# Hybrid encoder layer on one core: the first four row tiles in a hand-written order, seven idle products, a gain row spread over 97 partitions, one weight cast moved, and the last residual kept in PSUM

## The chip, the cores and the metric

The kernel runs on one core of a Trainium2 chip. A core has a matrix engine (TensorE, PE in the profile, with its weight loads listed apart as PEld), a vector engine (VectorE, DVE), an activation engine (ScalarE, ACT), a general engine (GpSimd, POOL) and a queue engine that mostly issues transfers (SyncE, SP). Products are written into PSUM, eight banks of 128 partitions; all else lies in SBUF. Each engine executes its own instructions strictly in the order in which the program lists them for it, and waits on semaphores of the others; transfers are issued from the queues of SP, ACT and POOL. The metric is the device time of one execution in microseconds (us).

## The reference, cut to what matters

```python
n = rms_norm(x, mix_norm_g)
proj = n @ w_in                      # 512 x 4608
...                                  
h = x + merged @ w_out
h = h + memory_cross_attention(rms_norm(h, xattn_norm_g), memn, w_q, w_k, w_v, w_xo)
h = h + (silu(hn @ w_gate) * (hn @ w_up)) @ w_down      # hn = rms_norm(h, ffn_norm_g)
return rms_norm(h, final_norm_g)
# rms_norm(x, g) = x * rsqrt(mean(x*x, -1) + 1e-6) * g
```

There are 512 token rows of 1024 float32 numbers. `proj` is cut into an S5 branch, a gated branch with GELU and layer norm, and two sigmoid gates. The change touches the first line (the norm of `x`, and the first 512 columns of the product that feed the gated branch), the load order at `w_xo` and `w_gate`, and the last line.

## The kernel before, in words

**Tiles and halves.** The 512 rows are four row tiles of 128 (`NT`), the 1024 features eight blocks of 128 (`KD`). Each float32 operand of a product is split in two: `hi`, a copy rounded to fp32r (a CAST on ACT), and `lo`, the source minus `hi` (a TENSOR_TENSOR on DVE). A product is three matmuls (`mm3`, the matmul's line is L360): hi by hi, hi by lo, lo by hi. So a weight tile costs a transfer into `wraw` (three buffers), a cast `whi` on ACT and a difference `wlo` on DVE (L85 and L86 for all of them, three buffers each) before PE can use it.

**What sets the order.** `plan` is the list of all weight tiles in the order of their use. `next_w` takes the next one and thereby issues loads some tiles ahead (`LOADS` 3) and splits two tiles ahead (`SPLITS` 2). Around this, a scheduler arranges each engine's instructions by its own estimate of when each can run, except where `tc.keep_in_program_order` (`in_order`) pins an instruction to its place in the program. `side` holds the S5 branch as a generator (`s5_program`, with the parameter set-up in `s5_setup`, L622), of which `tick` gives out pieces between products.

**The first rows.** Six idle products of `ones` by `ones` (L558) run on PE first. `mix_norm_g` arrives as one row on one partition (`g_row`), and a product of a single row of `ones` with it spreads it over 128 partitions into PSUM (`pg`, L581); ACT copies it to SBUF (`g_mix`). A row tile `xt` is squared and summed in two halves on ACT (`sum_sq`, L486), the factor is made by two small DVE operations and a power on POOL (`rms_factor`, L495 to L497), DVE scales the tile (L585 for the first tile, L512 for the others), PE transposes it in eight blocks (`to_feat`, L520) into `ptr`, and ACT and DVE split that into `xn`, the operand of all of stage one. Row tiles 1 to 3 go through the same steps in a loop. Then `tokm(w_in, OFF_V, ...)` (L1031) runs over four weight tiles of `w_in`, each two feature blocks by 512 columns, and all four row tiles: 96 matmuls into four banks `pt`. After it come the `feat` products (`pf`). The transfers stand on SP's queue in this order: the gain, half of row tile 0 (the other half on ACT's queue), the first weight tile, row tile 1, the second weight tile, row tile 2, the third, row tile 3; after them the S5 parameters, the first of which is `slab<-in_s_log_step_dram`, whose exponential stands at L674.

**w_xo and w_gate.** The second half of `w_xo` is four plan blocks of two feature blocks each; the first two use the ordinary `whi`/`wlo` buffers, the other two go to places `s2` and `s4`. Then `plan_units` takes the first block of the last 256 columns of `w_gate` into place `s1`, ahead of everything else that it plans. In the profile these casts read `s<-wraw`, and the sums on the rows that follow each product are L1348 on DVE and L486 on ACT.

**The end.** The last product of `w_down` (`dx`, quadrant 4) ends with row tile 3. `finish_last(None, ...)` adds what `dx[1]` holds to the residual `h` (L1806); the last three weight tiles are then multiplied in two column halves into a fresh bank `pcut`, each half is added to `h` on DVE (L1806 again), squared and summed (L486), and after the second the square root (L1788), the reciprocal (L1789), the scaling (L1819 on ACT, L1823 on DVE) and the two last transfers follow.

## Time and profile before

| | |
|---|---|
| device time, median of 3 executions | 871.61 us (870.81 to 874.23) |
| device time of the profiled execution | 871.84 us |
| its span, first to last instruction | 870.1 us, so 1.74 us lie around it |
| PE, PEld busy | 859.9 us (99%), 767.3 us (88%) |
| DVE, ACT, POOL busy | 660.9 us (76%), 464.5 us (53%), 92.3 us (11%) |
| moved by DMA | 169.56 MB, mean 195 GB/s |

The span counts from the first instruction of the program to the last. A busy PE is not PE at its peak: matmuls are pipelined, and the row of one shows its whole passage, 389 ns for 512 columns, while in an unbroken series one starts each 227 ns. In the timeline a row gives the start in us, the duration (of all, where several were merged, as x2), engine, line, operation, what is written `<-` what is read, the shape, and in brackets how long the engine had been idle and what ended that. A window row gives, for a stretch, its length and the busy time and count of each engine; with a source line it counts that line's instructions alone. A group row gives the count, the busy sum, the mean duration in ns and the idle time in front. The wait list gives total, times, longest.

### The profile page before, as it was taken

What the parts mean: (1) busy time and instruction counts of PE and PEld (TensorE: products, weight loads), DVE (VectorE), ACT (ScalarE), POOL (GpSimd) and SP (SyncE); (2) the same over time, 40 slices, a digit from 0 to 9 for tenths busy, and PEclk for the clock granted to TensorE, in tenths of its full rate; (3) what the DMA queues carried; (4) which work ended last, traced back from release to release, by engine and by line L of the source; (5) the groups of instructions that cost most, each with busy time, mean ns of one, the idle gap of its engine ahead of it and who ended that gap; (6) DMA issues with size and microseconds to landing.
All of it is one profiled execution on the core that took longest, in us unless ns stands there. A gap on an engine that the chain in (4) does not pass through costs nothing.

```text
span 870.1 us, 14734 instructions
## 1 busy us (share of the span) xinstructions
PE 859.9 (99%) x5766; PEld 767.3 (88%) x5766; DVE 660.9 (76%) x1072; ACT 464.5 (53%) x693; POOL 92.3 (11%) x127
## 2 busy tenths in 40 slices
PE   8999999999999999999999999999999999999996
PEld 6787888888889988889899878999999999988875
DVE  5699885999857768668758755867877768899875
ACT  5643953244356544547556554655545455656574
POOL 1002200301021210100010001001111111000010
PEclk9999999999999999999999999999999999999999
DMA  8769556797655898725686545557899998366672
GB/s 246 197 181 299 111 160 178 175 248 194 169 174 174 259 284 265 248 97 194 215 269 169 147 130 161 146 149 194 205 237 237 214 227 224 92 190 203 197 239 96
DMA packets 115464, 169.56 MB, mean 195 GB/s; under 512 B 9265, under 2 KB 80449, under 8 KB 115266
## 3 DMA queue, kind: packets, MB, share of 16 engines
q1 hardware_dynamic: 94722, 138.50, 48.5%
q0 software_dynamic: 20384, 29.60, 20.7%
q8 instruction: 45, 0.74, 0.3%
q10 hardware_dynamic: 288, 0.52, 0.2%
q14 instruction: 25, 0.20, 0.1%
HBM read 159.71 MB, written 48.73 MB: 240 GB/s over the span
## 4 chain that ended last, share of the span: by engine, by line
PE 95%; DMA 2%; DVE 1%; ACT 1%; SPq 1%; issue 0%; ACTq 0%; DVEq 0%
PE pf L360 26%; PE pt L360 16%; PE px L1158 13%; PE dx L360 6%; PE pq L1158 6%; PE dq L360 3%; PE pv L1158 3%; PE bx L1158 3%; PE qx L1158 3%; PE dv L360 2%; PE pz L892 2%; PE qv L1158 1%; PE po L360 1%; PE psc L360 1%; PE py L948 1%; PE qq L1158 1%
## 5 line engine op out<-in xcount | busy, mean ns | idle before, releaser
L85 ACT CAST whi<-wraw 128x1024 fp32r<-128x1024 f32 (+1 forms) x145 | 148.7, 1025 | 161.8 <-PE pf L360 51.4
L86 DVE TENSOR_TENSOR wlo<-wraw,whi 128x1024 fp32r<-128x1024 f32 (+1 forms) x145 | 172.1, 1188 | 60.5 <-ACT whi L85 59.7
L360 PE MATMUL pf<-xn,whi 128*128 128x512 f32 x448 | 140.2, 392 | 0.0
L360 PEld LDWEIGHTS pf<-xn,whi 128*128 128x128 f32 x448 | 83.7, 188 | 17.1 <-issue 0.2
L360 PE MATMUL pf<-xn,wlo 128*128 128x512 f32 x224 | 87.6, 392 | 0.0
L1158 PE MATMUL px<-fn,whi 128*128 128x256 f32 x480 | 83.4, 277 | 0.0
L1158 PEld LDWEIGHTS px<-fn,whi 128*128 128x128 f32 x480 | 72.5, 188 | 0.2
L86 DVE TENSOR_TENSOR wlo<-b,whi 128x1024 fp32r<-128x1024 f32 x40 | 48.9, 1222 | 26.1 <-ACT whi L85 26.0
L85 ACT CAST whi<-b 128x1024 fp32r<-128x1024 f32 x40 | 42.1, 1053 | 48.6 <-PE px L1158 27.8
L1158 PE MATMUL px<-fn,wlo 128*128 128x256 f32 x240 | 66.4, 277 | 0.0
L1158 PE MATMUL pq<-s,whi 128*128 128x256 f32 x320 | 55.0, 276 | 0.0
L360 PE MATMUL dx<-whi,s 128*128 128x512 f32 x166 | 52.2, 391 | 0.4 <-DVE h L1831 0.4
L86 DVE TENSOR_TENSOR wlo<-t,whi 128x1024 fp32r<-128x1024 f32 x30 | 36.7, 1224 | 18.4 <-ACT whi L85 18.4
L85 ACT CAST whi<-t 128x1024 fp32r<-128x1024 f32 x30 | 31.6, 1054 | 34.3 <-PE pv L1158 11.4
L360 PEld LDWEIGHTS pf<-xn,wlo 128*128 128x128 f32 x224 | 42.1, 188 | 8.8 <-issue 0.2
L1158 PEld LDWEIGHTS pq<-s,whi 128*128 128x128 f32 x320 | 48.2, 188 | 0.0
L360 PE MATMUL pt<-whi,xn 128*128 128x512 f32 x128 | 44.5, 414 | 1.3 <-ACT xn L85 1.1
L1158 PEld LDWEIGHTS px<-fn,wlo 128*128 128x128 f32 x240 | 45.1, 188 | 0.0
L1158 PE MATMUL pq<-s,wlo 128*128 128x256 f32 x160 | 44.2, 276 | 0.0
L360 PEld LDWEIGHTS dx<-whi,s 128*128 128x128 f32 x166 | 31.1, 188 | 7.4 <-issue 0.8
L360 PE MATMUL dx<-wlo,s 128*128 128x512 f32 x83 | 32.3, 391 | 0.1
L277 POOL DMA_DIRECT2D dsum<-in_w_down_dram x12 | 13.3, 1109 | 174.7 <-DMA dsum<-in_w_down_dram 171.0
(456 smaller groups left out, 2217.7 us busy)
## 6 DMA issues: line engine op xcount, KB each, us to landing
wraw<-in_w_in_dram SPq DMA_DIRECT2D x36, 512.0 KB, 4.8
dsum<-in_w_down_dram SPq DMA_DIRECT2D x20, 512.0 KB, 5.9
wraw<-dsum SPq DMA_DIRECT2D x20, 512.0 KB, 4.0
b<-in_w_gate_dram SPq DMA_DIRECT2D x15, 512.0 KB, 5.4
b<-in_w_up_dram SPq DMA_DIRECT2D x15, 512.0 KB, 4.8
wraw<-in_w_down_dram SPq DMA_DIRECT2D x15, 512.0 KB, 4.6
dsum<-in_w_down_dram POOLq DMA_DIRECT2D x10, 512.0 KB, 8.0
dsum<-dsum POOLq DMA_DIRECT2D x10, 512.0 KB, 8.6
```

The costliest lines, as they stand in the source:

```text
L85: hi = nc.scalar.copy(dst_hi, src)
L86: lo = nc.vector.tensor_tensor(dst_lo, src, dst_hi.bitcast(F32), ALU.subtract)
L277: plan[j + step][1].append((0, lambda d=dst, x=more: nc.gpsimd.dma_start(d, x, accum_op=ALU.add)))
L360: m = nc.tensor.matmul(ps, a[x], b[y], start=start and i == 0, stop=stop and i == 2, skip_group_check=free)
L892: nc.tensor.matmul(ps[:, g, :], wt[:, g, :], u[:, o * GO + g, :], start=True, stop=True)
L948: in_order(nc.tensor.matmul(ps[64 * j:64 * j + 64, :, :, h, :].rearrange("p q d c -> p d q c"), a, b, start=k == ks[0], stop=k == ks[2], t ...
L1158: nc.tensor.matmul(ps[:, j, :], a[x], b[y], start=start and j == k == i == 0, stop=k == 3 and i == 2, skip_group_check=True)
```

## The change

Four parts.

1. **First rows.** `first_rows` now builds all four row tiles from a hand-written string of steps, all pinned: `sq` squares a half, `ms` scales the first half's sum on DVE, `rt` takes the square root on ACT (the power on POOL is gone), `rc` the reciprocal on DVE, `sc` scales a half from the spread gain in PSUM, `pt` transposes four blocks, `hi` and `lo` split them, `whi` and `wlo` split half a weight tile, `p` is three matmuls of one row tile with one feature block of one of the first three weight tiles (`p121` is row 1, weight tile 2, block 1), `idle2` and `idle5` are two and five idle products. The gain arrives on partition 96 of a tile whose partitions 0 to 95 are set to zero, and is spread by a product of 97 rows. The first products run between the preparations; what `tokm` did is written out with the rest of them. The first two weight tiles are loaded in two halves each, and the third stands ahead of row tiles 2 and 3.
2. **S5 set-up.** The exponential of `log_step` is issued where the step is loaded.
3. **w_gate's first cast** gets a dependency in order alone on the cast of the second block of `w_xo`.
4. **The end.** The residual of the last row tile's right half is added to what `dx[1]` holds into two free banks `dv` (`seed_last`), the last products accumulate onto these, and squares and scaling read PSUM.

```diff
     def split(dst_hi, dst_lo, src):
...
+        return hi
...
-        split(hi, lo, src)
+        cast[0] = split(hi, lo, src)
         return hi, lo

+    cast = [None]
+
+    def behind(ins, first):
+        tc.add_manual_dep(ins.ins, first.ins.name, mybir.DependencyInfo(
+            mybir.DependencyClass.NoSync, mybir.DependencyReason.DATA), reason="order of the casts")
...
-            ins = nc.sync.dma_start(got["raw"], block(w, kb, k, c0, n))
-            if ordered:
-                in_order(ins)
+            for i in range(0, k, k // parts):
+                ins = nc.sync.dma_start(got["raw"][:, i:i + k // parts], block(w, kb + i, k // parts, c0, n))
+                if ordered:
+                    in_order(ins)
...
-            plan_block(w_gate, 4 * i, 4, FS, 256, place=i + 1, ordered=True)
+            plan_block(w_gate, 4 * i, 4, FS, 256, place=i + 1, ordered=True,
+                       then=None if i else lambda ins: behind(ins, xo_cast[0]))
...
-    plan_tok(w_in, OFF_V, KD)
+    plan_tok(w_in, OFF_V, KD, parts=2)
...
+    xo_cast = []
     for i in range(4):
-        plan_block(w_xo, 2 * i, 2, 512, 512, place=(None, None, 2, 4)[i], ordered=True)
+        plan_block(w_xo, 2 * i, 2, 512, 512, place=(None, None, 2, 4)[i], ordered=True,
+                   then=xo_cast.append if i == 1 else None)
...
-    idle = aux("idle", (P, P))
+    pg = [bank("pg") for i in range(2)]
+    pt = {t: bank(f"pt{t}") for t in range(NT - 1)}
...
-    nc.scalar.activation(warm, mhalf, AF.Square)
+    nc.scalar.activation(warm, ones[:, 0:1], AF.Sqrt)
...
+    G_ROW = 96
+    g_row = np_.tile([P, D], F32, tag="gain", name="g_row", bufs=2)
+    nc.vector.memset(g_row[0:G_ROW], 0.0)
+    in_order(nc.sync.dma_start(g_row[G_ROW:G_ROW + 1], mix_norm_g))
     nc.scalar.dma_start(xt[:, 0, HALF[1]], x[0:P, HALF[1]])
-    for t in range(1, NT):
-        load_raw(t - 1)
-        nc.sync.dma_start(xt[:, t, :], x[t * P:(t + 1) * P])
+    in_order(nc.sync.dma_start(xt[:, 0, HALF[0]], x[0:P, HALF[0]]))
+    for row, blocks in ((0, (0,)), (1, (1, 2)), (2, ()), (3, ())):
+        if row:
+            in_order(nc.sync.dma_start(xt[:, row, :], x[row * P:(row + 1) * P]))
+        for i in blocks:
+            load_raw(i)
...
+        def pg_(i):
+            in_order(nc.tensor.matmul(pg[i], ones[0:G_ROW + 1, :], g_row[0:G_ROW + 1, HALF[i]], start=True, stop=True))
+        def rt(t):
+            in_order(nc.scalar.activation(sums[t][:, 0:1], sums[t][:, 1:2], AF.Sqrt, bias=roots.pop(t), scale=1.0 / D))
...
+    ORDER = """
+        pg0 sq00 sq01 ms0 pg1 rt0 rc0 sc00 idle2 pt00 whi00 hi00 wlo00 whi01 lo00 sc01 sq10 idle5 p000 whi10
+        pt01 ms1 wlo01 sq11 wlo10 p001 rt1 whi11 rc1 p010 sc10 hi01 wlo11 pt10 whi20 sc11 hi10 p011 sq20 lo10
+        pt11 wlo20 p100 sq21 ms2 lo01 p101 rt2 sq30 rc2 sc20 p110 hi11 ms3 sq31 pt20 sc21 p020 hi20 lo11 pt21
+        whi21 lo20 p111 rt3 hi21 wlo21 p200 rc3 p021 sc30 p201 lo21 p120 sc31 pt30 p210 hi30 pt31 lo30 p211
+        hi31 bank3 p300 lo31 p121 p301
+    """
...
-        A_.activation(stp, ls, AF.Exp)
+        in_order(A_.activation(stp, ls, AF.Exp))
...
+    def seed_last(ps):
+        for i in range(2):
+            in_order(nc.vector.tensor_tensor(last[i], h[:, NT - 1, last_cols[i]], ps[:, 256 * i:256 * i + 256], ALU.add))
...
-    finish_last(None, dx[1])
+    seed_last(dx[1])
...
-        p = aux("pcut", (P, 256))
         for c, ops_ in held:
-            rows_product({1: p}, 4, c, ops_, (1,), slice(256 * i, 256 * i + 256), c == CHUNKS - HELD, c == CHUNKS - 1, True)
-        finish_last(i, p)
+            rows_product({1: last[i]}, 4, c, ops_, (1,), slice(256 * i, 256 * i + 256), False, c == CHUNKS - 1, True)
+        finish_last(i)
```

How this moves instructions is seen at three places. First PE at the program's start, before (L558 idle, L581 the spread of the gain, L520 transposes of `xt`, L360 products):

```order
L558 MATMUL idle<-ones 128x128 x6
L581 MATMUL pg<-g_row,ones 128x512 x2
L520 MATMUL ptr<-ident,xt 128x128 x8
L360 MATMUL pt_263<-whi,xn 128x512
L360 MATMUL pt_263<-wlo,xn 128x512
```

and now (L573 idle, L608 the gain, L635 transposes, L374 products; the idle products write the bank of the third `pt`):

```order
L573 MATMUL pt_111<-ones 128x128 x6
L608 MATMUL pg<-g_row,ones 128x512 x2
L573 MATMUL pt_111<-ones 128x128 x2
L635 MATMUL ptr<-ident,xt 128x128 x4
L573 MATMUL pt_111<-ones 128x128 x5
L374 MATMUL pt_109<-whi,xn 128x512
L374 MATMUL pt_109<-wlo,xn 128x512
L374 MATMUL pt_109<-whi,xn 128x512
L635 MATMUL ptr<-ident,xt 128x128 x4
```

The first products of row tile 0 now stand between the transposes of its two halves, and idle products fill the places ahead of the first transposes and of the first product.

Second, ACT at `w_xo`, before (L486 squares of a finished row tile; of the two `s` casts the second is `w_gate`'s; `whi<-wraw` is the second block of `w_xo`):

```order
L486 ACTIVATE sq,hss<-h 128x512 [waits DVE_49]
L85 CAST s_5468<-wraw 128x1024 [waits DMAHW0_49]
L85 CAST whi<-wraw 128x1024 [waits DMAHW2_49,PE_49]
L486 ACTIVATE sq,hss<-h 128x512 [waits DVE_49,Activation_49]
L85 CAST whi<-b_5447 128x1024 [waits DMAHW1_49,PE_49]
```

and now:

```order
L500 ACTIVATE sq,hss<-h 128x512 [waits DVE_49,Activation_49]
L85 CAST whi<-wraw 128x1024 [waits DMAHW4_49,PE_49]
L85 CAST s_5478<-wraw 128x1024 [waits DMAHW2_49]
L85 CAST whi<-b_5457 128x1024 [waits DMAHW3_49,PE_49]
L500 ACTIVATE sq,hss<-h 128x512 [waits DVE_49,Activation_49] x3
```

The two casts change places, and the squares of the third row tile come ahead of both.

Third, DVE at the end, before:

```order
L1806 TENSOR_TENSOR h<-h,dx_8067 128x512
L1866 TENSOR_TENSOR h<-h,dx_8066 128x512
L1789 RECIPROCAL r<-ms 128x1
L1823 SCALAR_TENSOR_TENSOR h<-h,r,g_o 128x512
L1806 TENSOR_TENSOR h<-h,pcut 128x256
L1774 SCALAR_TENSOR_TENSOR msq<-ss,msq 128x1
```

and now:

```order
L1890 TENSOR_TENSOR dv_8215<-h,dx_8077 128x256
L1890 TENSOR_TENSOR dv_8216<-h,dx_8077 128x256
L1950 TENSOR_TENSOR h<-h,dx_8076 128x512
L1869 RECIPROCAL r<-ms 128x1
L1908 SCALAR_TENSOR_TENSOR h<-h,r,g_o 128x512
L1854 SCALAR_TENSOR_TENSOR msq<-ss,msq 128x1
L1908 SCALAR_TENSOR_TENSOR h<-dv_8215,r,g_o 128x256
L1908 SCALAR_TENSOR_TENSOR h<-dv_8216,r,g_o 128x256
```

The two additions of `pcut` behind the last products are gone; one addition ahead of them became two of half the width, and the last scaling became two of half the width.

More of the change, by code (lines that the diff above doesn't have):

```diff
@@ L670, in s5_setup @@
         st["c"] = (cr, ci)
-        stp, a, rho, th, n, sn, hs, cs = (small() for _ in range(8))
-        A_.activation(stp, ls, AF.Exp)
+        a, rho, th, n, sn, hs, cs = (small() for _ in range(7))
         V.tensor_tensor(a, lr, stp, ALU.mult)
@@ L1822, in write @@
         (nc.gpsimd if t < 2 else nc.sync).dma_start(rows[:, cs], hg[:, t, :])
[L1823 to L1825 removed]
+        for src, cols in zip(last, last_cols) if t == NT - 1 else ((h[:, t, hs], hs),):
+            scaled = nc.vector.scalar_tensor_tensor(h[:, t, cols], src, r, g_o[:, cols], ALU.mult, ALU.mult)
+            if pinned[0]:
+                in_order(scaled)
         (nc.gpsimd, nc.gpsimd, nc.sync, nc.scalar)[t].dma_start(rows[:, hs], h[:, t, hs])
```

133 lines of the change are left out of this document (82 added, 51 removed).

## The prediction

> **What bounds the kernel now.** I read the chain of waits first, then PE's waits, then the stretches around them in the timeline. The chain's shares by engine:
>
> ```profile
> PE 95%; DMA 2%; DVE 1%; ACT 1%; SPq 1%; issue 0%; ACTq 0%; DVEq 0%
> ```
>
> The end is PE's list of instructions, so a change counts only where it shortens the work on PE, speeds it up, or removes one of PE's few stops. The largest stops, as total, times, longest:
>
> ```profile
> PE pt L360 <- ACT xn L85: 1.1, 1, 1.1
> PE pt L360 <- DVE wlo L86: 0.7, 1, 0.7
> ```
>
> The first lies in the first rows (17.34 below), the second at `w_xo` (520.22 below). All else that can be won is the speed of the first products and what stands behind the last one. For the speed, windows of L360 alone (length, PE busy and count, PEld, granted clock):
>
> ```profile
> 9.60:13.50 3.90, 3.85 (x8) 2.61 (x9) 1.00 1.05 349
> 18.10:22.00 3.90, 3.90 (x18) 3.19 (x17) 1.00 0.88 231
> 29.20:42.50 13.30, 10.69 (x43) 7.58 (x42) 1.00 0.63 149
> ```
>
> The granted clock is 1.00 in every row, yet 8 products fill 3.9 us in the first and 18 in the second: a product every 0.43 us (3.4/8) until about 13.5, every 0.22 to 0.23 afterwards. The clock column does not show this slowness; only the spacing does. I use 0.227 for the fast step and 0.427 for the slow one.
>
> **Part 1, the start.** The rows of before:
>
> ```profile
> 3.92 3.78 PE L581 MATMUL pg<-g_row,ones 1*128 1x512 f32 x4
> 4.25 0.63 ACT L486 ACTIVATE sq<-xt 128x512 f32<-128x512 f32 x1 [1.59 <-DMA xt<-in_x_dram]
> 6.72 0.75 DVE L585 SCALAR_TENSOR_TENSOR xt<-xt,r,pg 128x512 f32<-128x512 f32 x1 [0.76 <-ACT g_mix L583]
> 8.54 1.12 PE L520 MATMUL ptr<-ident,xt 128*128 128x128 f32 x4
> 9.65 0.80 PE L360 MATMUL pt<-whi,xn 128*128 128x512 f32 x1
> 15.16 1.03 PE L520 MATMUL ptr<-ident,xt 128*128 128x128 f32 x8
> 16.59 0.23 ACT L674 ACTIVATE slab<-slab 128x32 f32<-128x32 f32 x1 [0.58 <-DMA slab<-in_s_log_step_dram]
> 17.34 0.50 PE L360 MATMUL pt<-whi,xn 128*128 128x512 f32 x1 [1.15 <-ACT xn L85]
> 42.51 0.62 PE L360 MATMUL pf<-xn,whi 128*128 128x512 f32 x2
> ```
>
> From the first product (9.65) to the first `pf` (42.51) pass 32.9 us. The work in them, at the fast step: 96 products, 96 x 0.227 = 21.8. 24 transposes of rows 1 to 3: eight pass in 1.03, of which the last one's passage is about 0.27, so (1.03 - 0.27)/7 = 0.11 each, 2.6 together. The S5 set-up's small transposes: the third window is 13.3 long and 43 products take 9.8 of it, which leaves 3.5, and 3.8 with one that lies earlier. Sum 28.2. The other 4.7 us are the slow step until 13.5 (8 x 0.2 = 1.6), the stop of 1.15 at 17.34, where ACT stood with the exponential of the step (16.59, waiting for a transfer) ahead of the cast that PE needed, and small waits for weight tiles. All three are what the change addresses: products of row 0 begin between its transposes, PE is kept occupied ahead of them, and the exponential leaves ACT's first rows.
>
> What happens instead, by the list of steps. The gain still takes four passes of which one lasts about 0.85 (3.78 for four, overlapping): the half that `sc00` needs is ready near 6.0. Row 0's halves land at about 3.5 (2.8 after an issue at 0.75 on ACT's queue) and 4.2; the one that lands first is now squared first, so both are squared near 5.0, and with root and reciprocal (0.3 and 0.2) the factor is there near 5.5. So the gain decides: `sc00` starts near 6.1, 0.6 before the scaling at 6.72, since the copy into `g_mix` is gone. The idle products' price has a row:
>
> ```profile
> L558 PE MATMUL idle<-ones 128*128 128x128 f32 x12 | 2.9, 434 | 1.1 <-DVE mhalf L481 1.1
> ```
>
> Six of them (two passes each) cost 2.9 slow, 0.24 a pass; `idle2` and `idle5` are 4 and 10 passes: 0.9 and 2.4 slow, and at the fast spacing of a transposition (0.11) 0.4 and 1.1. They fill time in which PE would wait for the scaling and for the cast, so fast they cost nothing; slow, `idle5` stands up to 1 us in front of the first product. That is the first unknown: whether PE is fast at 7 or at 13.5.
>
> Fast from about 6.7 (my choice, because the spread is then 97 rows and not one, and PE is busy without gaps from about 1): the spread ends 7.1, `idle2` 7.5, four transposes 8.0, the cast of half a row 8.8 (0.6 for 512 columns), `idle5` covers to 9.05, first product 9.05. Then only row 0 and row 1 feed PE until row 2 arrives. Rows of `xt` land thus:
>
> ```profile
> 2.05 0.47 SPq L573 DMA_DIRECT2D xt<-in_x_dram  x1
> 3.07 0.47 SPq L573 DMA_DIRECT2D xt<-in_x_dram  x1
> DMA to landing us min/median/max: 2.8/7.2/11.4
> ...
> xt<-in_x_dram SPq DMA_DIRECT2D x3, 512.0 KB, 8.8
> ```
>
> Row 1 lands near 2.05 + 7.2 = 9.2 and row 3 (last issue, the maximum) near 4.6 + 11.4 = 16.0; the median of the three whole rows is 8.8, so row 2 lands at 3.07 + 8.8 = 11.9. The third weight tile now stands ahead of row 2, one transfer of the same size, and row 2 and the weight tile ahead of it came within 2.6 of row 1, so row 2 comes 1.3 to 1.8 later, near 13.7. Squares twice 0.63, the read of the sum 0.2, root 0.3, reciprocal 0.2, scaling 0.75: its transposes start about 16.8. Up to there the list has 21 products and 16 transposes, 21 x 0.227 + 16 x 0.11 = 6.5 us of 7.75, so 1.3 us stay idle. Behind it all is at hand: 75 x 0.227 = 17.0, 16 transposes 1.75, set-up 3.8, joints 0.3: 16.8 + 22.9 = 39.7. Against 42.51 that is **-2.8 us**.
>
> Bounds. If the step stays slow until 13.5 as before, `idle2` ends 8.4, the first product is at about 11.4, five products pass up to 13.5 with the transposes between them, and 91 to 93 products are left: 13.5 + 21.1 + 2.6 + 3.8 + 0.6 = 41.6: a gain of 0.9, less up to 0.2 for slow transposes: -0.7. If nothing waits from 9.05 on: 9.05 + 21.8 + 3.05 (28 transposes) + 3.8 + 0.4 = 38.1: -4.4. The zeroing of 96 rows of `g_row` has no row in before: between nothing and 1.2 (a DVE pass of 1024 columns, 518.94 below), on DVE while the gain is still in flight; hidden, since the spread begins only at 3.92.
>
> The exponential now has a table of its own behind the roots:
>
> ```profile
> L562 ACT ACT_TABLE_LOAD x1 | 1.3, 1283 | 1.2 <-PEq L1893 1.2
> ```
>
> 1.28 us on ACT, which comes after the first rows' casts, while PE has 20 us of products at hand; at nothing, or 1.3 if it stood ahead of a cast that PE waits for.
>
> **Part 3, `w_xo`.** ACT and DVE before:
>
> ```profile
> 516.12 1.05 ACT L85 CAST s<-wraw 128x1024 fp32r<-128x1024 f32 x1 [2.14 <-DMA wraw<-in_w_gate_dram]
> 516.19 0.39 PE L360 MATMUL pt<-whi,ot_lo 128*128 128x512 f32 x1
> 517.07 1.05 ACT L85 CAST whi<-wraw 128x1024 fp32r<-128x1024 f32 x1
> 517.20 1.23 DVE L86 TENSOR_TENSOR s<-wraw,s 128x1024 fp32r<-128x1024 f32 x1 [2.75 <-ACT s L85]
> 518.94 1.22 DVE L86 TENSOR_TENSOR wlo<-wraw,whi 128x1024 fp32r<-128x1024 f32 x1
> 520.22 0.50 PE L360 MATMUL pt<-wlo,ot_hi 128*128 128x512 f32 x1 [0.69 <-DVE wlo L86]
> 541.35 1.03 ACT L85 CAST s<-wraw 128x1024 fp32r<-128x1024 f32 x1
> ```
>
> ACT stands 2.14 us for `w_gate`'s transfer, then casts it, and only then `w_xo`'s block; DVE does the same, and `wlo` is done at 520.16, where PE waits. Turned round, the cast of `w_xo` waits for its buffer, which the product at 516.19 gives back (516.58): cast 516.6 to 517.65, difference 517.7 to 518.9, before PE is through the `whi` products (519.4). The stop of 0.69 and the ramp around it go: PE's last `whi` product starts 519.13, and 0.227 later would come the next, instead of 520.22: **-0.85 us**, between -0.6 and -0.9. Behind it stands `w_gate`'s first block about 2 us later; it gives its raw buffer back 1 to 2.5 us later, and so the next loads of `w_gate` are issued later, but their casts come only up to 541.35, some 20 us on. Without that cover it would cost what it is late, 2 us.
>
> **Part 4, the end.**
>
> ```profile
> 863.31 0.28 PE L360 MATMUL pcut<-whi,s 128*128 128x256 f32 x1
> 863.76 0.16 DVE L1774 SCALAR_TENSOR_TENSOR msq<-ss,msq 128x1 f32<-128x1 f32 x1 [0.57 <-ACT sq L486]
> 863.84 0.42 DVE L1806 TENSOR_TENSOR h<-h,pcut 128x256 f32<-128x256 f32 x1
> 864.29 0.42 ACT L486 ACTIVATE sq<-h 128x256 f32<-128x256 f32 x1 [0.56 <-DVE h L1806]
> 864.83 0.29 ACT L1788 ACTIVATE ms<-ss,msq 128x1 f32<-128x1 f32 x1
> 865.36 0.75 DVE L1823 SCALAR_TENSOR_TENSOR h<-h,r,g_o 128x512 f32<-128x512 f32 x1
> 866.14 0.36 ACTq L1826 DMA_DIRECT2D out_dram<-h  x1
> ```
>
> The last product ends at 863.59. Before, DVE adds 256 columns (863.84 to 864.26), ACT squares from 864.29. Now ACT can square from 863.65: 0.64 earlier. The scaling was one of 0.75; two of 256 columns at 0.42 with some overlap take 0.8 together: 0.05 to 0.1 given back. **-0.55 us**, between -0.35 (if squares from PSUM take 0.1 longer and the two scalings do not overlap) and -0.64. The seeds are one addition turned into two of 0.42 on DVE six microseconds before the end, and the products that accumulate on them are the last, some 1.5 us behind; at nothing, and 0.4 if they came late.
>
> **Sum.** -2.8 - 0.85 - 0.55 = -4.2 on the profiled 871.84: 867.6. The median shown, 871.61, is 0.23 lower: forecast 867.5, -0.47%.
>
> **The rivals.**
>
> *The step stays slow as long as before* (0.14). The start gives 0.7 instead of 2.8: 871.6 - 2.1 = 869.5 or a little over, 869.6. For it: before, PE was occupied from 1 us by idle products, the spread and transposes, and the products at 9.65 were still slow; nothing in that row says that seven more idle products will do it. Against it: the spread of one row is 3.78 us of it, and it now drives 97 rows. The Trainium skill ("TensorE: Matmul & The Clock Gate", "Part 1: The HAM clock gate") says that a window of some 3.4 us of sustained activity opens the clock, whatever is issued; by it before should have been fast by about 8 us, and the trace disagrees: the transposes at 8.54 and the products until 13.5 are at the slow spacing, so either one-row products do not count as activity or the windows fell badly. By that page's "Part 4: PE-mode transpose", transposes do not count either, and the change would then rest on the idle products and the spread alone.
>
> *The gain of the start is given back further on* (0.10). DVE is full for a long time:
>
> ```profile
> 60.00:70.00 10.00, 10.00 (x102) 7.78 (x101) 9.90 (x10) 2.51 (x5) 0.00 (x0) 1.00 1.02 301
> 59.86 1.21 DVE L86 TENSOR_TENSOR wlo<-wraw,whi 128x1024 fp32r<-128x1024 f32 x1
> 64.49 0.39 PE L360 MATMUL pt<-wlo,xn 128*128 128x512 f32 x1
> 241.79 2.07 DVE L936 COPY ss<-zh 64x1008 f32<-64x1008 f32 x2
> 247.67 0.66 PE L948 MATMUL py<-e,ss 128*64 128x128 f32 x8
> ```
>
> From 60 to 70 DVE works 9.90 of 10 us; a `wlo` is made at 61.07 and used at 64.49, a slack of 3.4. PE 2.8 earlier still finds it, 4.4 earlier does not. The scan's copies end at 243.86, and `py` reads them at 247.67, slack 3.8, of which 2.8 would be used. If DVE's list does not move forward with PE's, up to 2 us come back as a stop at one of the two: 869.5. Against it: DVE starts its part of the first rows earlier as well.
>
> *Row 3 lands late and the fixed order makes everyone wait* (0.10, the case on the other side). All four rows stand in one pinned list, and ACT's `sq30` and `sq31` precede `hi11` and `hi20`, which PE's next products need; before, the scheduler put such squares where the row was expected. Rows 2 and 3 are now last on SP's queue, behind a gain, two half tiles more and the third tile. Row 3 landed at 16.0, and up to 16.5 my list does not wait for it; each later microsecond is one lost. Break-even is 16.5 + 4.1 = 20.6; landing at 23 gives 867.5 + 6.5 = 874.0, and 25 is the point from which it shows as slower. For it: two more transfers than before share the queue, and 8.8 to 11.4 us to land show it backed up. Against: the bytes ahead of row 3 are the same, and whole transfers landed 1.3 apart. The Trainium skill ("DMA: Bandwidth & Descriptors", "Anatomy of one DMA — SWDGE (gpsimd) path") gives each transfer a fixed part of about 2.0 us beside its bytes; were that paid one after another, two more would put row 3 at 20 and the time, an estimate, at 871; transfers landing 1.3 apart disagree, the fixed part overlaps.
>
> **How the numbers follow.** 0.66 for the forecast, own range 866.0 to 868.8: the start between -1.6 and -4.2 round its -2.8. 0.14, 0.10 and 0.10 for the rivals. A difference of 0.5%, 4.36 us, is about what a measurement of this kernel tells from no change; faster means under 867.25, slower over 875.97. Half of the forecast's case lies under 867.25: 0.33. Slower is the half of the third rival in which row 3 lands after 25: 0.05. The rest, 0.62, is within 0.5%. The range 865.9 to 870.6 takes in the first two rivals and the start's bounds with little left out below; above it lies the third rival, and a part of the second where both its stops fall due.
>
> **What would show it.** The spacing of L374's products before 13.5: 0.23 right, 0.43 the first rival. The first product near 9.05 and the first `pf` near 39.7; no stop of 1.15 for `xn` behind an exponential. No stop for `wlo` near 517. Behind the last product no DVE addition, and the square at once. The stretch at 57 to 62 and `py` near 244 without new stops, or the second rival holds. ACT idle on a transfer of `xt` ahead of `sq30` means the third. I am wrong altogether if PE shows stops after the first 40 us that before does not have, or if the first `pf` is later than 42.5.

## The result and the profile after

| | before | changed |
|---|---|---|
| device time, median of 10 executions each | 871.79 us (869.87 to 876.73) | 867.96 us (866.33 to 869.90) |
| ratio of the times, 95% interval | | 0.9953 (0.9937 to 0.9969) |
| the profiled execution, and its span | 871.84, 870.1 us | 867.03, 865.2 us |

The kernel is 0.47% faster, close to the forecast of 867.5. The profiled execution gained a little more than the medians do: 4.8 us against 3.8. Where that lies is found by following the same products through both traces. Each number is how much earlier PE is in the changed kernel; "first pf by wlo" is used because two `pf` products now stand some 5 us ahead of the others in PE's list.

| place in the program | start before | start after | PE ahead by |
|---|---|---|---|
| first product of all | 9.65 | 7.77 | 1.88 |
| first `pf` by `wlo` | 42.96 | 38.97 | 3.99 |
| a product of `qx` | 434.18 | 430.51 | 3.67 |
| first `wlo` product behind `w_xo`'s stop | 520.22 | 515.72 | 4.50 |
| first `wlo` product behind the stop in `w_down` | 849.71 | 845.79 | 3.92 |
| last product | 863.31 | 859.37 | 3.94 |
| last issue on ACT's queue | 866.14 | 861.62 | 4.52 |

So in these two profiles four microseconds come from the start, 0.8 from `w_xo`, 0.6 from the end; 0.3 are lost on the way to 434, and 0.6 between `w_xo` and the last products. The rest of the 4.9 us of span, 0.4, lies behind the last issue.

Two profiles are two executions, and the start of the kernel before is not the same in each. A second profile of that same start (the kernel with parts 3 and 4 alone, below) has its first `pf` by `wlo` at 41.59; against that one the start gains 2.6 and not 4.0. The medians say 3.8 in all. Less 0.57 for the end, and with nothing measured for part 3 (below), some 3.3 us are left for the start and the exponential: an estimate from these numbers.

The chain of waits of the changed kernel, by engine:

```profile
PE 95%; DMA 1%; DVE 1%; ACT 1%; issue 1%; POOL 0%; SPq 0%; DVEq 0%; ACTq 0%; POOLq 0%
```

It is still PE's list. PE's largest waits (total, times, longest):

```profile
PE pt L573 <- DVE ones L493: 1.1, 1, 1.1
PE dx L374 <- DVE wlo L86: 0.6, 1, 0.6
PE ptr L635 <- DVE xt L629: 0.4, 2, 0.3
```

The first of them lies ahead of PE's first instruction and is there before the change too. The 1.1 us for `xn` and the 0.7 us for `wlo` at `w_xo` are gone; a wait of 0.6 in `w_down` is larger than before. The start in the timeline:

```profile
3.79 1.99 PE L608 MATMUL pg<-g_row,ones 97*128 97x512 f32 x4
...
6.27 0.63 PE L635 MATMUL ptr<-ident,xt 128*128 128x128 f32 x4
...
7.77 0.48 PE L374 MATMUL pt<-whi,xn 128*128 128x512 f32 x1
...
14.95 0.63 ACT L500 ACTIVATE sq<-xt 128x512 f32<-128x512 f32 x1 [0.26 <-DMA xt<-in_x_dram]
...
38.97 0.39 PE L374 MATMUL pf<-xn,wlo 128*128 128x512 f32 x1
```

The spread takes 2.0 us instead of 3.8, four transposes 0.63 instead of 1.12: PE is fast inside the spread already. The trace holds a record of the granted clock, which begins, at full clock, at 3.99 here and at 13.54 in the kernel before; that is where the spacing turns from slow to fast in each. For the time ahead of its first record a window row prints 1.00 for want of one, which is why the clock column could not show the slow start. ACT waits 0.26 for row 3 at 14.95. At `w_xo` the two casts have changed places and `wlo`'s product follows the one before it without a stop:

```profile
513.02 1.03 ACT L85 CAST whi<-wraw 128x1024 fp32r<-128x1024 f32 x1
513.96 1.04 ACT L85 CAST s<-wraw 128x1024 fp32r<-128x1024 f32 x1
...
515.49 0.39 PE L374 MATMUL pt<-whi,ot_hi 128*128 128x512 f32 x1
515.72 0.39 PE L374 MATMUL pt<-wlo,ot_hi 128*128 128x512 f32 x1
```

At the end ACT squares PSUM 0.04 us behind the last product (859.37 + 0.28 = 859.65), and no addition stands between:

```profile
859.37 0.28 PE L374 MATMUL dv<-whi,s 128*128 128x256 f32 x1
859.69 0.38 ACT L500 ACTIVATE sq<-dv 128x256 f32<-128x256 f32 x1 [0.44 <-PE dv L374]
...
860.72 0.88 DVE L1908 SCALAR_TENSOR_TENSOR h<-dv,r,g_o 128x256 f32<-128x256 f32 x2
861.62 0.35 ACTq L1911 DMA_DIRECT2D out_dram<-h  x1
```

### The profile page after: what moved, and what is told of

It reads as the page before. It is cut to its first block, busy times and chain, and to the rows that moved or that the text cites. A ratio compares the mean times of both kernels' runs of the same rounds, so it can differ in the third digit from the quotient of the medians.

```text
span 865.2 us, 14764 instructions
## 1 busy us (share of the span) xinstructions
PE 856.6 (99%) x5780; PEld 766.9 (89%) x5780; DVE 660.4 (76%) x1075; ACT 466.1 (54%) x698; POOL 91.6 (11%) x123
## 4 chain that ended last, share of the span: by engine, by line
PE 95%; DMA 1%; DVE 1%; ACT 1%; issue 1%; POOL 0%; SPq 0%; DVEq 0%; ACTq 0%; POOLq 0%
PE pf L374 27%; PE pt L374 17%; PE px L1238 13%; PE pq L1238 6%; PE dx L374 5%; PE dq L374 3%; PE pv L1238 3%; PE bx L1238 3%; PE qx L1238 3%; PE dv L374 2%; PE pz L958 2%; PE qv L1238 1%; PE po L374 1%; PE psc L374 1%; PE py L1014 1%; PE qq L1238 1%
## 5 line engine op out<-in xcount | busy, mean ns | idle before, releaser
L85 ACT CAST whi<-wraw 128x1024 fp32r<-128x1024 f32 x141 | 145.3, 1030 | 163.0 <-PE pf L374 55.5
L86 DVE TENSOR_TENSOR wlo<-wraw,whi 128x1024 fp32r<-128x1024 f32 x141 | 168.3, 1196 | 64.9 <-ACT whi L85 64.3
L374 PE MATMUL pf<-xn,whi 128*128 128x512 f32 x448 | 140.2, 393 | 0.0
L374 PEld LDWEIGHTS pf<-xn,whi 128*128 128x128 f32 x448 | 83.5, 188 | 16.8
L374 PE MATMUL pf<-xn,wlo 128*128 128x512 f32 x224 | 87.6, 391 | 0.0
L374 PE MATMUL dx<-whi,s 128*128 128x512 f32 x166 | 52.2, 391 | 0.4 <-DVE h L1916 0.4
L85 ACT CAST whi<-t 128x1024 fp32r<-128x1024 f32 x30 | 31.6, 1054 | 34.6 <-PE pv L1238 11.4
L374 PEld LDWEIGHTS pf<-xn,wlo 128*128 128x128 f32 x224 | 42.1, 188 | 8.6
L374 PE MATMUL pt<-whi,xn 128*128 128x512 f32 x128 | 43.1, 403 | 0.0
L374 PEld LDWEIGHTS dx<-whi,s 128*128 128x128 f32 x166 | 31.1, 188 | 7.3 <-issue 0.8
L374 PE MATMUL dx<-wlo,s 128*128 128x512 f32 x83 | 32.3, 391 | 0.6 <-DVE wlo L86 0.6
```

What stands on the lines that cost most here:

```text
L85: hi = nc.scalar.copy(dst_hi, src)
L86: lo = nc.vector.tensor_tensor(dst_lo, src, dst_hi.bitcast(F32), ALU.subtract)
L374: m = nc.tensor.matmul(ps, a[x], b[y], start=start and i == 0, stop=stop and i == 2, skip_group_check=free)
```

## The experiments

Ratios are to the kernel before, executed beside them. The last two columns are of the one profiled execution: where the record of the granted clock begins, at full clock (PE is slow ahead of it), and the start of the first `pf` by `wlo`. The kernel before has 13.54 and 42.96 there.

| kernel | median us (executions) | ratio, 95% interval | clock record from | first `pf` by `wlo` |
|---|---|---|---|---|
| changed | 867.96 (10) | 0.9953 (0.9937 to 0.9969) | 3.99 | 38.97 |
| changed, again | 867.40 (6) | 0.9944 (0.9926 to 0.9963) | 5.57 | 39.05 |
| before with parts 3 and 4 | 870.76 (10) | 0.9992 (0.9978 to 1.0006) | 11.57 | 41.59 |
| before, spread of 97 rows | 871.58 (10) | 1.0002 (0.9987 to 1.0018) | 5.52 | 45.22 |
| changed, spread of 1 row | 869.62 (10) | 0.9968 (0.9952 to 0.9984) | 13.77 | 42.43 |
| changed, spread of 33 rows | 870.11 (10) | 0.9977 (0.9963 to 0.9992) | 4.50 | 38.84 |
| changed, no `idle2`, `idle5` | 868.11 (5) | 0.9959 (0.9946 to 0.9972) | 5.26 | 39.00 |
| changed, 1 row and no `idle2`, `idle5` | 870.17 (10) | 0.9985 (0.9975 to 0.9994) | 15.13 | 41.98 |
| changed without part 2 | 872.60 (10) | 1.0003 (0.9991 to 1.0015) | 5.77 | 44.24 |
| changed without part 3 | 866.99 (6) | 0.9943 (0.9925 to 0.9960) | 7.04 | 39.76 |
| changed, row 3 late | 878.82 (4) | 1.0069 (1.0042 to 1.0096) | 4.22 | 50.56 |
| changed, `t` early | 867.02 (5) | 0.9937 (0.9921 to 0.9954) | 6.78 | 39.62 |
| changed, `t` early, scaling moved | 867.13 (6) | 0.9945 (0.9927 to 0.9963) | 6.28 | 39.38 |

### Parts 3 and 4 alone

The edit is the change's own diff for `w_gate`'s first cast and for the end, put into the kernel before.

> The kernel before with parts 3 and 4 alone; the start is untouched. Theory: at w_xo the step of 1.08 us between two products near 519 shrinks below 0.4 (0.85 won by the sum, 0.83 seen in the changed kernel), and from the end of the last product to the last issue on ACT's queue pass 1.97 us, as in the changed kernel, and not 2.55. First pf at 42.5 as before. Time 871.8 - 0.85 - 0.55 = 870.4. Rival: what is won at w_xo comes back at the stop for wlo near 849 (the changed kernel stands 0.58 longer there than the kernel before), since w_down's tiles come at their own pace: then the last product is less than 0.4 earlier than 863.6 and the time is 871.0 to 871.8.

The median moved 1.1 us, with an interval that still holds no change. The last product to the last issue took 2.26 (866.69 to 868.95) instead of 2.83 (starts of both): part 4 is worth 0.57. Between 430 and 550 the profiled execution, which was the slowest of its ten, shows what else happened. First, one transfer of a weight tile came late, ahead of a cast on ACT:

```profile
300.31 1.04 ACT L85 CAST whi<-wraw 128x1024 fp32r<-128x1024 f32 x1 [5.27 <-DMA wraw<-in_w_proj_b_dram]
```

It took 9.1 us to land where the same transfer took 4.0 in the kernel before, and PE stood 2.4 us. It was issued ahead of anything that the edit touches, so I take it for chance. Ordinary products stand on both sides of that stop, and behind it PE ran at half clock:

```profile
301.89 0.58 PE L1172 MATMUL bx<-yb_hi,whi 128*128 128x256 f32 x1 [2.39 <-ACT u L1190]
```

```profile
301.89:305.04 3.15, 3.15 (x14) 3.15 (x15) 0.50 0.42 127
```

These products come 0.21 us apart, and 0.11 apart ahead of the stop and from 305.2 on; the record of half clock runs from 301.70 to 305.12. Then `w_xo`'s stop was gone (the step between the two products was 1.09 us before and is 0.23, so 0.86 won), and a new stop stood at the transposes of `xs`:

```profile
539.83 0.66 PE L534 MATMUL ptr<-ident,xs 128*128 128x128 f32 x4 [1.23 <-ACT full L540]
```

That is not where the expectation's rival looked (849). It led to the experiments on part 3 below.

### What the start rests on: rows of the spread, idle products, the list

One row instead of 97:

```diff
-    nc.vector.memset(g_row[0:G_ROW], 0.0)
-    in_order(nc.sync.dma_start(g_row[G_ROW:G_ROW + 1], mix_norm_g))
+    in_order(nc.sync.dma_start(g_row[0:1], mix_norm_g))
...
-            in_order(nc.tensor.matmul(pg[i], ones[0:G_ROW + 1, :], g_row[0:G_ROW + 1, HALF[i]], start=True, stop=True))
+            in_order(nc.tensor.matmul(pg[i], ones[0:1, :], g_row[0:1, HALF[i]], start=True, stop=True))
```

> The changed kernel with the gain spread from one row, as before, all else kept. Theory A (the number of rows in the spread decides the speed of PE at the start): the four passes take 3.8 us again instead of 2.0, the first half of the gain is ready near 5.7 instead of 4.8, the first product comes at 9 to 10, and products follow each other at 0.43 until 12 or later; first pf at 41 to 42, time 870 to 871. Theory B (the idle products or the unbroken list do it): only the later gain counts, first product near 9, products at 0.23 from the first one on, first pf 39.5 to 40, time 868.5 to 869. Theory C (the order of the list alone): spread 2.0 and all times as in the changed kernel, first pf 39.0, 868.

Theory A held in the profile, but for the first product, which came later than its 9 to 10; the median, 869.62, lies a little under its 870 to 871:

```profile
3.92 3.78 PE L607 MATMUL pg<-g_row,ones 1*128 1x512 f32 x4
7.63 1.22 PE L573 MATMUL pt<-ones 128*128 128x128 f32 x4
...
9.50 2.34 PE L573 MATMUL pt<-ones 128*128 128x128 f32 x10
11.49 0.77 PE L374 MATMUL pt<-whi,xn 128*128 128x512 f32 x1
```

The idle products themselves are slow (2.34 for ten passes instead of 1.28) and push the first product to 11.49; the spacing turns fast near 13.8, and the first `pf` is 3.5 us later than in the changed kernel. But the ten times reach from 865.92 to 872.42, and the lowest is below the lowest of the changed kernel's ten. Of that execution there is no trace, so whether an early start can happen with one row, and only more seldom, is not shown.

No idle products, 97 rows:

```diff
-pg0 sq00 sq01 ms0 pg1 rt0 rc0 sc00 idle2 pt00 whi00 hi00 wlo00 whi01 lo00 sc01 sq10 idle5 p000 whi10
+pg0 sq00 sq01 ms0 pg1 rt0 rc0 sc00 pt00 whi00 hi00 wlo00 whi01 lo00 sc01 sq10 p000 whi10
```

> The changed kernel without idle2 and idle5, spread from 97 rows. Theory A (rows of the spread): PE is fast without them, transposes 0.11 apart, first product at 7.5 to 7.8, products 0.23 apart, first pf 38.7 to 39.2, time 867.5 to 868.2. Theory B (idle products): products at 0.43 until 12 or so, first pf 40 to 41, time 869 to 870.

Theory A again: first product 7.78, first `pf` 39.00, the same within 0.03 us as with them. The seven idle products do nothing here that can be seen. With both edits:

> The changed kernel with the gain from one row and without idle2 and idle5. Theory A: like the one-row kernel, the first product up to 1 us earlier or equal, since slow idle products stood in front of it; slow spacing until 12 or later, first pf 41 to 42, time 870 to 871. Theory B: slow spacing to 13.5 as in the kernel before, first pf 41 to 42; it differs from A only in that the one-row kernel with idle products was fast. Theory C: first pf 39.0, 868.

The first product came at 9.42, at the slow spacing until about 15, first `pf` 41.98. So the new list with neither aid is worth about 1.1 us of the median (from 871.84, the kernel before beside it, to 870.17, less the 0.57 of the end), with whatever parts 2 and 3 add in it. This kernel and the one above it in the table differ in the rows of the spread alone, and their intervals lie apart (0.9946 to 0.9972 with 97 rows, 0.9975 to 0.9994 with one): that is the plainest evidence in times that the rows count. With the idle products in place, the intervals of one row and 97 overlap.

33 rows, by the edit `G_ROW = 32`:

> The changed kernel with the gain on partition 32 of a tile with 32 rows of zeros, so that the spread multiplies 33 rows instead of 97. Theory A1 (any product of enough rows will do): as in the changed kernel, four passes in 2.0 us, products 0.23 apart from the first, first pf 39.0. Theory A2 (it goes by how much of the array is at work): the passes stay slow (3.8 us for four, 0.85 each) or the products do, slow spacing to 12 or so, first pf 40 to 42.4, time 869 to 870.

The profile shows A1: four passes in 2.25, first product 8.13, first `pf` 38.84. The median says otherwise: the profiled execution was the fastest of its ten (866.98), and their median, 870.11, is that of the one-row kernel. A single profile would have misled here. It also says little of 33 rows by itself: the record of full clock begins at 4.50, only 0.6 us after this spread's first pass (3.92) and behind 2.9 us of idle products that every kernel here has. The same holds of the changed kernel's own profile, 0.2 us into its spread. What the profiles show together is that all nine with 97 rows have full clock at 3.99 to 7.04 and all four with one row at 11.57 to 15.13. Why, and whether there is a threshold between one row and 97, is not shown.

97 rows in the kernel before, all else unchanged:

```diff
-    g_row = np_.tile([1, D], F32, tag="gain", name="g_row", bufs=2)
-    nc.sync.dma_start(g_row, mix_norm_g)
+    g_row = np_.tile([P, D], F32, tag="gain", name="g_row", bufs=2)
+    nc.vector.memset(g_row[0:96], 0.0)
+    nc.sync.dma_start(g_row[96:97], mix_norm_g)
```

> The kernel before with the gain spread from 97 rows (96 of them zero), all else as before. Theory A (the rows of the spread open PE's speed, and that is what the change's start won): the four passes take 2.0 us and the products from the first one on come 0.23 apart; the eight slow products save 8 x 0.2 = 1.6 and the spread 1.9, of which the part that row 1's late transposes (17.34 in the kernel before) do not swallow reaches the first pf: 40 to 41.3 instead of 42.5 (or 41.1 in the other profile of the same start), time 870 to 871. Theory B (spread and new list are both needed: without the list PE is fast but waits for the exponential and row 1): fast spacing, yet the first pf at 41.5 to 42.5 with a longer stop near 15 to 17, time 871.3 to 871.8.

Theory B's mechanism and its time, with a first `pf` (45.22) that it missed. PE was fast from the first product, then stood for the exponential and row 1, and was slow again behind it. The wait in the timeline, and windows of L360 over the time before, behind and later (the column before the last two is the granted clock):

```profile
17.98 0.50 PE L360 MATMUL pt<-whi,xn 128*128 128x512 f32 x1 [2.06 <-ACT xn L85]
```

```profile
9.40:11.90 2.50, 2.46 (x7) 1.08 (x7) 1.00 1.03 398
19.70:22.60 2.90, 2.90 (x8) 2.31 (x7) 0.50 0.95 267
23.10:26.00 2.90, 2.00 (x9) 1.31 (x7) 1.00 0.84 259
```

Here the clock column shows it: 0.50, half speed, on record from 19.17 to 22.58. In this execution, what the spread won was lost there. It was one of the slower of its ten, though (874.45, their median 871.58), so that the half speed is also what kept the median where it was is not shown. One wait is the same in this profile and in that of the kernel before: ACT can do the exponential only once its parameter has landed (17.22 here, 16.59 there), and what PE wins ahead of that it spends in waiting.

### Part 2, the exponential

```diff
-        in_order(A_.activation(stp, ls, AF.Exp))
...
         a, rho, th, n, sn, hs, cs = (small() for _ in range(7))
+        A_.activation(stp, ls, AF.Exp)
```

> The changed kernel with part 2 undone: the exponential of log_step is left to the scheduler, which puts it among the first rows on ACT, ahead of row 2's root, with two loads of tables (1.28 us each) around it. Theory: ACT waits there for the parameter's transfer, which in the changed kernel is issued behind all rows and lands later than row 3, and all later casts with it: PE stops 3 us or more near 13 to 20, first pf 41.5 to 44, time 870.5 to 873. Rival (the transfer has long landed and ACT has room): only the tables' 2.6 us on ACT, PE at most 1 us later, 868 to 869.

Of the edits that undo a part of the change this was the dearest: 872.60, the whole gain. ACT first:

```profile
15.40 1.28 ACT L740 ACT_TABLE_LOAD   x1 [1.10 <-DMA slab<-in_s_log_step_dram]
16.70 0.23 ACT L740 ACTIVATE slab<-slab 128x32 f32<-128x32 f32 x1
16.95 1.28 ACT L621 ACT_TABLE_LOAD   x1
```

1.10 of waiting, two table loads and the exponential hold ACT from 14.3 to 18.2, because the roots of the new list need another table than the exponential. PE waits behind them, and then is at half speed again (on record from 19.42 to 22.83):

```profile
19.61 1.09 PE L635 MATMUL ptr<-ident,xt 128*128 128x128 f32 x4 [3.76 <-issue]
```

```profile
20.30:22.50 2.20, 1.64 (x4) 0.95 (x4) 0.50 0.72 182
23.20:25.40 2.20, 2.20 (x11) 1.84 (x10) 1.00 0.97 272
```

The first `pf` is 5.3 us later: 3.8 of stop and 1 to 1.5 of slow products and transposes. The rival, 1 us at most, fell.

### Row 3 late: the prediction's slower case

```diff
+        if row == 3:
+            in_order(nc.sync.dma_start(xt[:, row, :], x[row * P:(row + 1) * P]))
```

> The changed kernel with row tile 3 loaded twice, the second time once the first has landed, so that the row that ACT's list waits for comes some 3 to 5 us later; what stands behind it on SP's queue (S5 parameters, weight tiles) is issued later too. Theory (the third rival of the prediction: every us past the point at which the list needs the row is one lost, and more where PE falls back to the slow spacing): ACT stands ahead of sq30 from about 15 to 18 or 20, PE stops 3 to 5 us there, then 8 to 12 products at 0.43; first pf 42.5 to 46, time 871.5 to 875. Against it: the list has enough work ahead, PE stops less than 1.5 and the time is below 869.5.

The delay was larger than meant: the second load was issued at 17.61, and ACT could square row 3 at 24.33 instead of 14.95.

```profile
24.33 0.63 ACT L500 ACTIVATE sq<-xt 128x512 f32<-128x512 f32 x1 [9.66 <-DMA xt<-in_x_dram]
```

```profile
25.95 1.11 PE L637 MATMUL ptr<-ident,xt 128*128 128x128 f32 x4 [8.80 <-DVE xt L631]
```

```profile
26.70:31.50 4.80, 4.79 (x11) 3.78 (x12) 0.50 0.37 125
```

9.4 us of delay made the kernel 11.4 us slower than the changed one executed beside it (878.82 against 867.40): 8.8 of stop, and 11 products in the 4.8 us behind it, where 21 fit, which is 2.3 more. The record of half clock runs from 21.28 to 31.52, so a part of it lies inside the stop. So the mechanism is real, and dearer than one for one; in the changed kernel ACT waits 0.26 for the row, and no stop of PE follows from it.

### Part 3: what the order of the casts costs further on

> The changed kernel with the load of w_gate's tile t issued one place earlier on SP's queue, ahead of the tile whose issue waits for the raw buffer that part 3 gives back later. Theory: the four kernels with part 3 show a stop of 0.29 to 1.39 at the transposes of xs near 531 that the kernel before does not have, because POOL's next row, an adding transfer into t, waits for t to land, and the power for the norm stands behind it in POOL's list. With t early POOL issues that transfer some us before the norm, the scaling follows its sum by 0.85 at most, and the stop is gone: 0.3 to 0.9 gained, 867.1 to 867.7 against the changed kernel's 868.0. Rival (the power waits for something else, the descriptors of the transfer or DVE): the stop stays and the time is 868.0.

```diff
-            (5, [(7, plain("t", b(0, 0))), (5, onto("t", b(0, 1))), ...
+            (5, [(8 if ordered and w is w_gate else 7, plain("t", b(0, 0))), (5, onto("t", b(0, 1))), ...
...
-        for j in range(i, min(i + FAR + 1, len(plan))):
+        for j in range(i, min(i + FAR + 2, len(plan))):
```

POOL in the changed kernel, the power for the third row's norm (`r<-ms,mhalf`) behind an adding transfer:

```profile
523.52 1.33 POOL L192 DMA_DIRECT2D t<-in_w_gate_dram  x1 [12.13 <-DVE h L1428]
524.53 0.92 POOL L511 TENSOR_TENSOR r<-ms,mhalf 128x1 f32<-128x1 f32 x1
...
528.84 0.54 POOL L511 TENSOR_TENSOR r<-ms,mhalf 128x1 f32<-128x1 f32 x1 [3.40 <-DVE ms L510]
```

and with `t` loaded early:

```profile
520.25 1.33 POOL L192 DMA_DIRECT2D t<-in_w_gate_dram  x1 [7.54 <-DMA t<-in_w_gate_dram]
525.58 0.55 POOL L511 TENSOR_TENSOR r<-ms,mhalf 128x1 f32<-128x1 f32 x1 [4.00 <-DVE ms L510]
```

The transfer is now out of the way 4 us ahead of the power, which follows its sum at once, and PE's stop at the transposes of `xs` is gone, as in the other kernel with `t` early. The brackets of the first block name DVE for the transfer's wait, but `t`'s landing is what it goes by: with `t` in its old place, the adding transfer starts 0.5 to 0.6 us after `t` has landed in every profile (`t` issued at 516.31 and landed 6.6 us later in the changed kernel).

All profiles together: with part 3 and `t` in its old place, seven of nine have the stop (some 0.3 to 1.4 us); without part 3, one of three (some 0.6, the kernel before with 97 rows). Part 3 is not its only cause; that it moves the odds fits these counts, few as they are, and the room that it leaves: `t` is issued 15.1 us ahead of those transposes with it (516.31 to 531.38) and 16.6 without it (519.43 to 536.01 in the kernel before), and takes 6.2 to 8.5 us to land. The power is late by as much as the transfer holds it: 0.37 us in the changed kernel, 1.61 in the kernel with parts 3 and 4 alone, nothing with `t` early. Whether the time gains is not shown: 867.02 against 867.96 and, later, 867.40, with intervals that overlap. The other side of it, part 3 undone:

```diff
-            plan_block(w_gate, 4 * i, 4, FS, 256, place=i + 1, ordered=True,
-                       then=None if i else lambda ins: behind(ins, xo_cast[0]))
+            plan_block(w_gate, 4 * i, 4, FS, 256, place=i + 1, ordered=True)
```

> The changed kernel with part 3 undone: w_gate's first cast again ahead of w_xo's second. Theory: the stop of 0.85 at w_xo returns, and the stop at the transposes of xs near 531 (0.29 to 1.39 in the kernels with part 3) goes, since w_gate's tile and t are issued earlier again: net 0 to 0.5 slower than the changed kernel, 868.0 to 868.5. Rival: part 3 is worth its whole 0.85, 868.8 to 869.0.

Neither: 866.99, not slower than the changed kernel beside it (867.40), and in its profile neither stop is there. `w_gate`'s transfer came in time:

```profile
512.85 1.05 ACT L85 CAST s<-wraw 128x1024 fp32r<-128x1024 f32 x1 [1.16 <-DMA wraw<-in_w_gate_dram]
```

It was issued at 507.58 and had landed within 5.3 us; in the kernel before it was issued at 509.87 and the cast began 6.25 later. The 0.85 of the prediction's row was one execution's; the kernel before with 97 rows shows 0.52 there. Part 3 covers a transfer that is sometimes 1 us late, seems to make a stop of up to 1.4 behind POOL likelier, and in the median is worth nothing that was measured: 866.99 and 867.40 are of six executions each, and a gain of under 1 us could hide there.

### A version to beat both

```diff
-pg0 sq00 sq01 ms0 pg1 rt0 rc0 sc00 idle2 pt00 whi00 hi00 wlo00 whi01 lo00 sc01 sq10 idle5 p000 whi10
+pg0 sq00 sq01 ms0 pg1 rt0 rc0 sc00 idle2 pt00 whi00 hi00 wlo00 sc01 whi01 lo00 sq10 idle5 p000 whi10
```

with `t` early as above, beside the changed kernel itself:

> The changed kernel with t early (as in the run before) and with DVE's scaling of row 0's second half moved ahead of the difference lo00, into the time in which DVE waits for the cast: the second transposes of row 0 then do not wait for it. Theory: the 0.15 to 0.4 us of PE waiting near 9 to 10 goes and with it the first pf comes 0.3 earlier: 866.7. Rival: row 1's arrival sets what follows, nothing but t early is won: 867.0.

> The changed kernel again, beside the three others on one chip: 868.0 from its ten earlier times, first pf between 38.8 and 39.7 if PE is fast from the first product on in this profile too, up to 41 if not.

867.13 against 867.40 and 867.02: the scaling's place wins nothing (the second transposes of row 0 wait no longer, those of row 1 still do). None of the three is shown to be faster than the changed kernel. I would keep `t` early because the stop at `xs` is missing in both profiles that have it, and not for its time.

## Why the prediction was right, point by point

**The bound.** PE's list, its stops and the speed of its first products: right. The two largest movements, without part 2 and with row 3 late, are accounted for by a stop of PE and slow products behind it. What part 3 and the 33 rows did in their profiles (a stop gone, an early full clock) does not show in their medians.

**The sum, -4.2.** The medians moved by 3.8. That the number came so close is in part luck: the start gave more than its 2.8 (4.0 against one profile of the old start, 2.6 against the other, some 3.3 by the medians), and the -0.85 of `w_xo` is in no median. The two errors nearly cancel.

**The start, -2.8.** Measured -4.0 up to the first `pf`, -3.7 after it, inside the bounds -0.7 to -4.4. The chosen end, fast from about 6.7, was right and a little shy: PE turned fast inside the spread (full clock on record from 3.99, passes at 3.79, 4.32, 4.75, 5.18), so the first product came at 7.77 and not 9.05. The term mis-sized is the spread, which I left at 3.8 us. Row 2's squares began at 12.81 where I put its landing at 13.7, and its transposes at 15.85, not 16.8. Of the two reasons given for the choice, rows of the spread and an unbroken list, the rows carry more of it: without the idle products 868.11 with 97 rows and 870.17 with one, and at 97 rows the idle products change nothing that was measured.

The Trainium skill ("TensorE: Matmul & The Clock Gate", "Part 1: The HAM clock gate") has the clock open after some 3.4 us of sustained activity, in windows that run freely. With 97 rows it opened between 3.99 and 7.04 in nine profiles, 2.9 to 6.0 us after PE's first pass at 1.06: that agrees roughly, 2.9 being a little short. With one row it opened between 11.57 and 15.13 in four profiles, although PE was occupied from 1.06 on: that does not, unless a product of one row counts as little, which no run here tests by itself. The prediction's line on the clock, that its column "does not show this slowness", read a 1.00 that stands where the trace has no record.

**What I had wrong inside the right number.** "All three are what the change addresses" treated the slow step (1.6), the exponential's stop (1.15) and the small waits as terms that add. They do not: each of the four stops of 2.06 us and more on record was followed by half speed. The rows alone won nothing (871.58), and without part 2 the rest won nothing (872.60). The exponential's stop of 1.15 is not in every execution of the old start either: in its second profile the parameter had landed in time, and PE did not stand for it. And I set the table at "1.28 us on ACT ... at nothing, or 1.3", with a place behind the first rows; it holds only because the exponential is pinned there.

**`idle2` and `idle5`.** "Fast they cost nothing; slow, `idle5` stands up to 1 us in front of the first product": both seen, the second in the one-row kernel: its first product came at 11.49, and at 9.42 without them, of which some 1.0 us is `idle2` (first transposes at 8.65 and 7.63) and some 1.05 `idle5`. That they win nothing, I did not say.

**`w_xo`, -0.85.** In the profiles -0.83 (changed) and -0.86 (parts 3 and 4 alone); in the medians nothing. The step that failed is "their casts come only up to 541.35, some 20 us on": I followed the later load of `w_gate` to its cast on ACT, and not to POOL's queue, where an adding transfer waits for `t` ahead of a power on which PE's transposes depend. And the row was taken for the rule: the transfer it rests on varies by 1 us from one execution to another.

**The end, -0.55.** -0.57 in every profile with part 4 (2.25 to 2.26 instead of 2.83 between the starts of last product and last issue).

**The rivals.** The slow step as long as before is what one row gives: 869.62 measured, 869.6 forecast. The gain given back further on: not at DVE's full stretch nor at the scan, where PE stayed 3.6 to 4.0 ahead, but some 0.3 at `xs` and up to 0.5 at a transfer in `w_down` (843.43, ACT 2.44 us idle for `wraw<-dsum`), 0.6 together by the table. Row 3 late: not the case; ACT waited 0.26, and when forced, 24.3 gave 878.8 where the sum of the prediction, 867.5 + (24.3 - 16.5), gives 875.3. Of the difference, 3.5, the half speed makes 2.3.

## What to carry to other kernels

A stop of PE of some 2 us or more costs its own length and then, in every case seen here, some microseconds at half speed, so early gains do not add: look for the one operation (here an exponential with a transfer and two tables behind it) that breaks the run of products, and move that first. When an operation is put later, follow every queue that it feeds, those that only issue transfers too, down to the next thing on the path. And take a stop that rests on when a transfer lands from more than one profile.

## What the runs showed of the hardware that I had not expected

Stops of PE of 2.06, 2.39 and 3.76 us each brought one stretch of half clock, on record for 3.41 or 3.42 us, and a stop of 8.80 one of 10.24. Stops of 1.15 (the kernel before) and 1.23 us (parts 3 and 4 alone) left PE fast; between 1.23 and 2.06 nothing was seen. Half clock does not set in at once: behind the stop of 2.06, PE resumed at 17.98 and the record of half clock starts at 19.17.

Ahead of the stop of 2.06 stand eight transposes, so that no product started for 3.6 us. By the Trainium skill ("TensorE: Matmul & The Clock Gate", "Part 4: PE-mode transpose") transposes do not count as busy, which fits this row. The stop of 2.39 has products right ahead of it and no transposes, so the transposes are not needed for the effect.
